# A two-block transformer forward pass on one core: the modulation vectors' operations, spread over two feed-forwards and held in VectorE's program order

## The chip, the cores and the metric

One NeuronCore of one Trainium2 chip runs the whole program. The metric is the device time of one execution in microseconds (us); the time before is the median of three runs. TensorE does the matrix products, VectorE and ScalarE the elementwise work, GpSimd a part of the elementwise work, and SyncE's queue issues the DMAs. Each engine works through its own instructions in order.

## The reference

Two transformer blocks follow each other. Block 1 (512 tokens and 16 meta tokens, width 1024) has three branches, an output projection, and a feed-forward with a squared ReLU:

```python
u = jnp.square(jax.nn.relu(rms_norm(x, norm2_w) @ w_up))     # 1024 -> 4096
return x + u @ w_down                                        # 4096 -> 1024
```

Block 2 is modulated by vectors that depend only on two inputs, `c` and `c_ctx`, not on the tokens. `m` has nine parts of 1024 values for the latent tokens, `mc` the same for 256 context tokens (of which only parts 0 to 4 are used here, since there is one layer):

```python
m  = jnp.split((jax.nn.silu(c) @ w_ada[l] + b_ada[l])[:, None, :], N_MOD, axis=-1)
mc = jnp.split(jax.nn.silu(c_ctx) @ w_ada[l] + b_ada[l], N_MOD, axis=-1)
x = _residual(x, _swiglu(_modnorm(x, g[0], m[0], m[1]), w1, w3, w2), g[1], m[2], HALF_STEP)      # first feed-forward
h_ctx = _residual(h_ctx, _swiglu(_modnorm(h_ctx, g[0], mc[0], mc[1]), w1, w3, w2), g[1], mc[2], HALF_STEP)
# then: projections with m[3], m[4]; two attentions; residual with m[5]; second feed-forward with m[6], m[7], m[8]
```

So parts 0 and 1 are wanted when block 2's first feed-forward begins, part 2 after it, and the rest later still.

## The kernel before, in words

All products are in float32 split into a high and a low part: each product is three matmuls (high by high, high by low, low by high), and every weight tile is split on the way in, the high part by ScalarE (L132), the low part by the engine that `lo_eng` names for even and odd chunks (L136; VectorE and GpSimd alternate in the stages of interest here). A weight unit is 128 output rows by 1024, in two chunks of 4 x 128 columns; three raw buffers and four split buffers are in rotation.

The class `Emitter` writes the instructions out in one order. It walks over a list of products (`_gemm`), and after each matmul it calls `tick` (L157) with an assumed time of that matmul: its columns / 2.4 + 3 ns, 216.3 ns for 512 columns. A generator that was given to `background` is advanced by one step (a slot) each time the sum of these assumed times reaches its pace; `drain` runs all that is left of it at once. After that a scheduler orders each engine's instructions anew: it may take an instruction ahead of others on its engine if its operands are there earlier in its own model, and it inserts the waits.

Block 1's feed-forward runs in four groups. In a group, eight units of `w_up` are multiplied (8 x 24 matmuls of 512 columns), each followed by `up_evac` (L1038): VectorE multiplies out of PSUM (L1045) and squares the ReLU (L1046), ScalarE writes the high part `uh`, and VectorE (odd units) or GpSimd (even units) the low part `ul` (L274). Then eight units of `w_down` are multiplied with all eight `uh`, `ul` of the group: their last of eight steps needs the output of the group's last `up_evac`. Four PSUM buffers are in rotation.

`ada_bg` (L975) computes the modulation vectors beside this feed-forward, on VectorE: 72 tiles of `w_ada` of 128 x 1024 are loaded (three buffers, SyncE's queue), and each is multiplied with silu(c) and summed along its row in one instruction (L995) that writes one column of `modc`; the first 40 tiles are also multiplied with silu(c_ctx). It has a pace of 2250 ns. At its end come the bias and the nine coefficient vectors `cf` (L1000 to L1013). Before the fourth group it is drained, and `ctx_ops` closes its pool `ad` and prepares the context tokens.

Block 2's first feed-forward (`ffn`, L1119, with tag f1) follows. It has three groups of 6, 8 and 8 hidden tiles; a tile has a unit of w1 and a unit of w3, each 24 matmuls on 258 and 24 on 512 columns, whose evacuations `e1`, `e3` end in the high part `hh` (ScalarE) and the low part `hl` (VectorE for the 512 columns, GpSimd for the 256). After a group come its products with w2, first on 256 and then on 512 columns. `f1_tail` holds the third group's products, with `update` (the residual and the next norm) beside them.

Of the kernel before, what the change touches and what calls it, by code (L numbers as in the profile page):

```python
# [6 lines left out]
F32 = mybir.dt.float32  # L7
F32R = mybir.dt.float32r
I32 = mybir.dt.int32
AF = mybir.ActivationFunctionType  # L10
ALU = mybir.AluOpType
# [3 lines left out]
D = 1024  # L15
# [243 lines left out]
def emit(tc, d, out, dbg=None, stop=None):  # L259
    nc = tc.nc  # L260
    V, A, G, T, SP = nc.vector, nc.scalar, nc.gpsimd, nc.tensor, nc.sync
    pools = Pools(tc)
    em = Emitter(tc)
# [4 lines left out]
    S = {"dram": dram}  # L268

    def act(o, i, f=AF.Copy, **kw):  # L270
        A.activation(o, i, f, **kw)

    def sub_lo(eng, lo, x, hi):
        eng.tensor_sub(lo, x, hi.bitcast(F32))  # L274
# [21 lines left out]
    def col(name, i=0, n=1):  # L296
        o = _PCOLS[name][0] + i
        return pc[:, o:o + n]
# [7 lines left out]
    def hilo(hi, lo, x, c):  # L306

        act(hi, x, scale=c)
        V.scalar_tensor_tensor(lo, x, c, hi.bitcast(F32), ALU.mult, ALU.subtract)
# [640 lines left out]
    AF0, A0C, B1X, B1C, A2X, A2C, B3, A4, B5 = range(9)  # L950

    def cf(i, k=None):
        t = S["cf"][:, i, :]
        return t if k is None else t[:, k:k + 1]

    def mod(k, s=0):
        return S["modc"][:, s, 8 * k:8 * k + 8]

    def open_f():
        for n in ("m2", "bina", "xhl"):  # L960
            pools.close(n)
        p = S["hlx"] = pools.open("hlx")
        S["XH"] = p.tile([128, KT, 514], F32R, name="XH")
        S["XL"] = p.tile([128, KT, 514], F32R, name="XL")
        S["modc"] = p.tile([128, 2, 72], F32, name="modc")
        S["cf"] = p.tile([128, 9, 8], F32, name="cf")
        S["R4"] = p.tile([128, 768], F32, name="R4")
        S["RF"] = p.tile([128, 512], F32, name="RF")
        p = S["hlc"] = pools.open("hlc")
        S["CH"] = p.tile([128, KT, 258], F32R, name="CH")  # L970
        S["CL"] = p.tile([128, KT, 258], F32R, name="CL")
        S["up"] = pools.open("up")
        S["ad"] = pools.open("ad")

    def ada_bg():  # L975

        p = S["ad"]
        sb = p.tile([128, 2, D], F32, name="sb")
        SP.dma_start(sb, d["cc"].partition_broadcast(128))
        act(sb, sb, AF.Silu)  # L980
        W, todo = [], list(range(72))

        def load():
            if todo:
                w = p.tile([128, D], F32, name="wa", tag="wa", bufs=3)
                SP.dma_start(w, d["wa"][todo.pop(0)])
                W.append(w)
        for _ in range(3):
            load()
        yield  # L990
        for j in range(72):
            w = W.pop(0)
            for s_ in ((1, 0) if j < 40 else (0,)):
                o = w if s_ == 0 else p.tile([128, D], F32, name="wx", tag="wx")
                V.tensor_tensor_reduce(o, w, sb[:, s_, :], 1.0, 0.0, ALU.mult, ALU.add,  # L995
                                       S["modc"][:, s_, j:j + 1])
                if s_ == 0:
                    load()
                yield
        V.tensor_add(S["modc"][:, 0, :], S["modc"][:, 0, :], col("bada", 0, 72))  # L1000
        V.tensor_add(S["modc"][:, 1, 0:40], S["modc"][:, 1, 0:40], col("bada", 0, 40))

        def gcol(i):
            return col("g", 8 * i, 8)
        for o, i, m_, s_ in ((AF0, 0, 1, 0), (A0C, 0, 1, 1), (A2X, 2, 4, 0), (A2C, 2, 4, 1), (A4, 4, 7, 0)):
            V.tensor_scalar_add(cf(o), mod(m_, s_), 1.0)
            V.tensor_mul(cf(o), cf(o), gcol(i))
        V.tensor_mul(cf(AF0), cf(AF0), col("final", 0, 8))
        for o, i, m_, s_, w in ((B1X, 1, 2, 0, 0.5), (B1C, 1, 2, 1, 0.5), (B3, 3, 5, 0, None), (B5, 5, 8, 0, 0.5)):
            V.tensor_mul(cf(o), mod(m_, s_), gcol(i))  # L1010
            if w is not None:
                V.tensor_scalar_mul(cf(o), cf(o), w)
        yield  # L1013

    def shift_cols(kx, kc):
        todo = [(S["XH"], S["XL"], 512 + i, mod(kx)) for i in range(2)]
        if kc is not None:
            todo += [(S["CH"], S["CL"], 0, mod(kx)), (S["CH"], S["CL"], 1, mod(kc, 1))]
        for h_, l_, o, m_ in todo:
            act(h_[:, :, o], m_)  # L1020
            sub_lo(V, l_[:, :, o], m_, h_[:, :, o])

    def ctx_ops():

        pools.close("ad")
        p = S["fp"]
        shift_cols(0, 0)
        for k in range(KT):
            c = p.tile([128, 256], F32, name="xr", tag="xr", bufs=3)
            SP.dma_start(c, d["cx"][:, k, :])  # L1030
            hilo(S["CH"][:, k, 2:258], S["CL"][:, k, 2:258], c, cf(A0C, k))
            squares(c, S["acc"][:, 0:256], k == 0, S["fpa"], G)
        tmp = S["fpa"].tile([128, 512], F32, name="sq", tag="sq", bufs=2)
        rnorm(S["R4"][:, 512:768], S["acc"][:, 0:256], D, tmp, gap=2800)
# [24 lines left out]
    def last_down(n, x):  # L1059
# [22 lines left out]
        em.after(1500, norms)  # L1082

    em.call(open_f)
    em.background(ada_bg, 2250)
    for g in range(4):
        if g == 3:
            em.drain()
# [30 lines left out]
    def ffn(tag, w1, w3, w2, mode, ntok, pool, Rk, down, head, tail):  # L1119


        st = {}
        grp = ((0, 6), (6, 8), (14, 8))

        def e1(j):
            def f(t0, n, ps, b):
                s_ = st[j, t0] = S[pool].tile([128, 512], F32, name="fs", tag="fs", bufs=3)[:, 0:n]
                V.tensor_mul(s_, ps, S[Rk][:, t0:t0 + n])  # L1128
                act(s_, s_, AF.Silu, bias=b)
            return f  # L1130

        def e3(j):
            def f(t0, n, ps, b):
                s_ = st.pop((j, t0))
                t = S[pool].tile([128, 512], F32, name="ft", tag="ft", bufs=2)
                V.tensor_mul(t[:, 0:n], ps, S[Rk][:, t0:t0 + n])  # L1136
                V.scalar_tensor_tensor(s_, t[:, 0:n], b, s_, ALU.add, ALU.mult)
                hh, hl = st["h"]
                act(hh[:, j, t0:t0 + n], s_)
                sub_lo(G if t0 else V, hl[:, j, t0:t0 + n], s_, hh[:, j, t0:t0 + n])  # L1140
            return f

        def newh():
            st["h"] = [S[pool].tile([128, KT, ntok], F32R, name="h" + e, tag="h" + e) for e in "hl"]

        for gi, (k0, nk) in enumerate(grp):
            em.call(newh)

            def pair(j, m, a=0, k0=k0):
                proj(w1[k0 + j], 128, m, e1(j), (tag, 1, a))  # L1150
                proj(w3[k0 + j], 128, m, e3(j), (tag, 3, a))

            def products(segs, gi=gi, k0=k0, nk=nk):
                for n in range(8):
                    em.gemm(w2[n][:, k0:k0 + nk, :], 128, lambda si: st["h"], segs,
                            lambda si, ps, n=n: down(gi, n, segs[si][0], segs[si][1], ps), kt=nk)

            for j in range(head(pair) if gi == 0 else 0, nk):
                pair(j, mode)
            if gi == 2:  # L1160
                tail(products)
            else:
                products([(512, 256), (0, 512)] if ntok == 768 else [(0, 512)])
# [88 lines left out]
        return 0  # L1252

    def f1_tail(products):
        products([(256, 512)])
        em.low_parts(V, V)
        em.call(lambda: shift_cols(3, 3))
        em.background(lambda: update(256, 768, S["fpa"], B1X, A2X, B1C, A2C, True), 1150)
        products([(0, 256)])
        em.drain()  # L1260

    em.call(open_f1)
    ffn("f1", d["w11"], d["w13"], d["w12"], XC, 768, "hid", "R4", f1_down, no_head, f1_tail)


# [20 lines left out]

    def open_kvp():
        pools.close("hid")
        p = S["kvp"] = pools.open("kvp")
        S["KH"] = p.tile([128, 2, 768], F32R, name="KH")  # L1290
        S["KL"] = p.tile([128, 2, 768], F32R, name="KL")
        S["Rkv"] = p.tile([128, 768], F32, name="Rkv")
        S["rkc"] = p.tile([128, 6], F32, name="rkc")
        S["akv"] = p.tile([128, 768], F32, name="akv")
        S["tmpk"] = p.tile([128, 768], F32, name="tmpk")
        S["krt"] = p.tile([32, 768], F32, name="krt")
        S["krs"] = p.tile([32, 2, 768], F32R, name="krs")
# [678 lines left out]
```

## Time and profile before

| | |
|---|---|
| median of 3 runs | 2831.26 us (2831.24 to 2832.66) |
| the profiled execution's own time | 2835.28 us |
| its span | 2833.3 us, mean granted TensorE clock 0.984 |
| TensorE matmul busy | 2736.0 us, 97% |
| TensorE weight load busy | 2405.3 us, 85% |
| VectorE busy | 1620.0 us, 57% |
| ScalarE busy | 1092.5 us, 39% |
| GpSimd busy | 849.9 us, 30% |
| DMA | 316.95 MB, mean 112 GB/s |

The busy time of TensorE is that of pipelined matmuls, so overlaps are in it. PE stands for TensorE, DVE for VectorE, ACT for ScalarE, POOL for GpSimd, SP for SyncE. A name like L995 is a line of the kernel. "<-" before an engine names what an engine's idle time ended with.

### The profile page before, as it was taken

To read this page: it belongs to the slowest core of one execution; us is meant where nothing else is said; L and a number is where in the kernel's file an instruction comes from. 1 tells how busy PE (TensorE), PEld (TensorE's weight loads), DVE (VectorE), ACT (ScalarE), POOL (GpSimd) and SP (SyncE) were. 2 spreads that over 40 slices of the span, in tenths; PEclk is the share of its full clock that TensorE was granted. 3 is DMA by queue.
4 is the path that set the end of the run, shared out by engine and by line. 5 is a ranking of instruction groups with operands and counts; after the bars stand their busy time and mean duration, and the time that the engine had idled before them with its cause. 6 is when DMAs were issued, how large, how long until landed. Compare 5 with 4: busy or idle time off the path is not lost.

```text
span 2833.3 us, 42915 instructions
## 1 busy us (share of the span) xinstructions
PE 2736.0 (97%) x16308; PEld 2405.3 (85%) x16308; DVE 1620.0 (57%) x3318; ACT 1092.5 (39%) x2201; POOL 849.9 (30%) x710
## 2 busy tenths in 40 slices
PE   9999999999999889899999999979999999899997
PEld 8889988888878667788888888868889998899897
DVE  6554422377757999555223233496576876834346
ACT  4333322445534222243222122354455665633233
POOL 0223323433324233242111112442333224323224
PEclk9999999999999999999999999989999999999998
DMA  4222222443225658332121221334643424332324
GB/s 136 73 68 91 96 97 93 129 125 102 83 93 191 205 195 295 114 108 68 53 75 60 61 66 60 93 117 156 179 102 103 133 62 162 133 97 90 93 94 127
DMA packets 115998, 316.95 MB, mean 112 GB/s; under 512 B 21680, under 2 KB 35376, under 8 KB 115536
## 3 DMA queue, kind: packets, MB, share of 16 engines
q1 hardware_dynamic: 115792, 314.21, 35.5%
q8 instruction: 129, 2.11, 0.3%
q14 instruction: 77, 0.63, 0.1%
HBM read 279.09 MB, written 13.83 MB: 103 GB/s over the span
## 4 chain that ended last, share of the span: by engine, by line
PE 80%; DVE 14%; issue 3%; ACT 2%; DMA 0%; POOL 0%; POOLq 0%; DVEq 0%; SPq 0%; ACTq 0%
PE psg L231 49%; PE pss L231 22%; DVE wlo L136 2%; DVE wa L995 2%; DVE wx L995 1%; PE pss L277 1%; PE pst L827 1%; PE pss L278 1%; PE pss L279 1%; PE pst L1731 1%; PE pst L1717 1%; PE pss L1528 1%; PE pst L824 0%; DVE ut L1045 0%; DVE mg L1224 0%
## 5 line engine op out<-in xcount | busy, mean ns | idle before, releaser
L136 POOL TENSOR_TENSOR wlo<-raw,whi 128x512 fp32r<-128x512 f32 (+1 forms) x442 | 580.1, 1313 | 1568.4 <-ACT whi L132 1527.4
L132 ACT ACTIVATE whi<-raw 128x512 fp32r<-128x512 f32 (+1 forms) x844 | 522.7, 622 | 927.8 <-PE psg L231 588.8
L136 DVE TENSOR_TENSOR wlo<-raw,whi 128x512 fp32r<-128x512 f32 (+1 forms) x402 | 314.0, 782 | 452.6 <-ACT whi L132 451.9
L231 PE MATMUL psg<-xl,whi 128*128 128x264 f32 (+2 forms) x1104 | 362.7, 329 | 0.9 <-DVE xl L403 0.9
L231 PE MATMUL psg<-xh,whi 128*128 128x264 f32 (+2 forms) x1104 | 361.4, 328 | 1.7 <-ACT whi L132 1.2
L231 PE MATMUL psg<-xh,wlo 128*128 128x264 f32 (+2 forms) x1104 | 361.7, 328 | 0.0
L231 PE MATMUL psg<-XH,whi 128*128 128x256 f32 (+3 forms) x984 | 308.2, 313 | 1.8 <-DVE ft L1136 1.0
L231 PE MATMUL psg<-XH,wlo 128*128 128x256 f32 (+3 forms) x984 | 308.2, 313 | 0.0
L231 PE MATMUL psg<-XL,whi 128*128 128x256 f32 (+3 forms) x984 | 307.8, 313 | 0.0
L231 PEld LDWEIGHTS psg<-xh,whi 128*128 128x128 f32 x1104 | 209.0, 189 | 18.8 <-ACT whi L132 1.4
L231 PEld LDWEIGHTS psg<-xl,whi 128*128 128x128 f32 x1104 | 209.1, 189 | 18.5 <-DVE xl L403 1.5
L231 PEld LDWEIGHTS psg<-xh,wlo 128*128 128x128 f32 x1104 | 209.2, 190 | 17.0 <-DVE wlo L136 0.2
L231 PE MATMUL pss<-XL,whi 128*128 128x256 f32 (+2 forms) x600 | 191.3, 320 | 6.1 <-DVE XL L1208 6.1
L231 PEld LDWEIGHTS psg<-XH,whi 128*128 128x128 f32 (+1 forms) x984 | 185.4, 188 | 11.5 <-issue 2.4
L231 PEld LDWEIGHTS psg<-XH,wlo 128*128 128x128 f32 (+1 forms) x984 | 185.8, 189 | 10.5 <-issue 0.2
L231 PEld LDWEIGHTS psg<-XL,whi 128*128 128x128 f32 (+1 forms) x984 | 185.8, 189 | 9.3
L231 PE MATMUL pss<-XH,wlo 128*128 128x256 f32 (+2 forms) x600 | 191.4, 319 | 1.2 <-DVE wlo L136 1.2
L231 PE MATMUL pss<-XH,whi 128*128 128x256 f32 (+2 forms) x600 | 190.9, 319 | 0.5 <-DVE fs L1128 0.5
L231 PEld LDWEIGHTS pss<-XL,whi 128*128 128x128 f32 x600 | 114.9, 192 | 14.3 <-DVE XL L1208 7.3
L231 PEld LDWEIGHTS pss<-XH,wlo 128*128 128x128 f32 x600 | 115.4, 192 | 10.1 <-DVE wlo L136 1.6
L231 PEld LDWEIGHTS pss<-XH,whi 128*128 128x128 f32 x600 | 114.9, 192 | 7.5 <-DVE fs L1128 0.7
L231 PE MATMUL pss<-hh,wlo 128*128 128x256 f32 (+1 forms) x296 | 101.8, 344 | 7.5 <-DVE wlo L136 7.5
(558 smaller groups left out, 6444.6 us busy)
## 6 DMA issues: line engine op xcount, KB each, us to landing
raw<-w SPq DMA_DIRECT2D x142, 512.0 KB, 3.3
raw<-wi SPq DMA_DIRECT2D x96, 512.0 KB, 3.3
wa<-wa SPq DMA_DIRECT2D x72, 512.0 KB, 4.2
raw<-wq SPq DMA_DIRECT2D x38, 512.0 KB, 3.5
raw<-wu SPq DMA_DIRECT2D x32, 512.0 KB, 4.2
raw<-wd SPq DMA_DIRECT2D x32, 512.0 KB, 4.1
raw<-wb SPq DMA_DIRECT2D x24, 512.0 KB, 3.2
raw<-wo SPq DMA_DIRECT2D x24, 512.0 KB, 4.0
```

The costliest lines, as they stand in the source:

```text
L132: s.nc.scalar.activation(h, raw, AF.Copy)
L136: eng.tensor_sub(l, raw, h.bitcast(F32))
L231: nc.tensor.matmul(out, l, r, start=(k == 0 and m == 0), stop=(k == it.kt - 1 and m == 2))
L277: T.matmul(o, wh, xh, start=first, stop=False)
L278: T.matmul(o, wh, xl, start=False, stop=False)
L279: T.matmul(o, wl, xh, start=False, stop=last)
L827: T.matmul(o, x[:, c, :], vs[:, c, :], start=False, stop=c == b and m == 1)
L995: V.tensor_tensor_reduce(o, w, sb[:, s_, :], 1.0, 0.0, ALU.mult, ALU.add, S["modc"][:, s_, j:j + 1])
L1528: T.matmul(ps[:, a:a + cw], q, k[:, c0:c0 + cw], start=m == 0, stop=m == 1)
L1717: T.transpose(ps[:, 128 * c:128 * c + 128], P_[:, 128 * (c0 + c):128 * (c0 + c) + 128], ident)
L1731: T.matmul(o[:, 0:256], v[:, c, :], x[:, c, :], start=c == 0 and m == 0, stop=c == 5 and m == 1)
```

## The change

The generator is started twice. The first time, beside block 1's feed-forward, it computes tiles 0 to 15 alone (parts 0 and 1, both inputs: 32 of the 112 operations of L995) at a pace of 8000 ns. The second time, beside block 2's first feed-forward, it computes tiles 16 to 71 (80 operations) at a pace of 4800 ns, and is drained before the products of the third group. Each call adds the bias to its own columns and makes the coefficients whose part it has. Every operation of L995 is wrapped in `keep_in_program_order`, which adds an edge without a wait behind the instruction that was written last on that engine, so that the scheduler can't issue it before that one. The loads have two buffers in place of three; the pool `ad` is opened before `up`, and stays open until `hid` is closed after block 2's first feed-forward.

```diff
+        S["ad"] = pools.open("ad")
         S["up"] = pools.open("up")
-        S["ad"] = pools.open("ad")
-
-    def ada_bg():
+
+    def ada_bg(j0, j1):
+
         p = S["ad"]
-        sb = p.tile([128, 2, D], F32, name="sb")
-        SP.dma_start(sb, d["cc"].partition_broadcast(128))
-        act(sb, sb, AF.Silu)
-        W, todo = [], list(range(72))
+        if j0 == 0:
+            S["sb"] = p.tile([128, 2, D], F32, name="sb")
+            SP.dma_start(S["sb"], d["cc"].partition_broadcast(128))
+            act(S["sb"], S["sb"], AF.Silu)
+        W, todo = [], list(range(j0, j1))
 
         def load():
             if todo:
-                w = p.tile([128, D], F32, name="wa", tag="wa", bufs=3)
+                w = p.tile([128, D], F32, name="wa", tag="wa", bufs=2)
                 SP.dma_start(w, d["wa"][todo.pop(0)])
                 W.append(w)
-        for _ in range(3):
-            load()
+        load()
+        load()
         yield
-        for j in range(72):
+        for j in range(j0, j1):
             w = W.pop(0)
             for s_ in ((1, 0) if j < 40 else (0,)):
                 o = w if s_ == 0 else p.tile([128, D], F32, name="wx", tag="wx")
-                V.tensor_tensor_reduce(o, w, sb[:, s_, :], 1.0, 0.0, ALU.mult, ALU.add,
-                                       S["modc"][:, s_, j:j + 1])
+                tc.keep_in_program_order(
+                    V.tensor_tensor_reduce(o, w, S["sb"][:, s_, :], 1.0, 0.0, ALU.mult, ALU.add,
+                                           S["modc"][:, s_, j:j + 1]))
                 if s_ == 0:
                     load()
                 yield
-        V.tensor_add(S["modc"][:, 0, :], S["modc"][:, 0, :], col("bada", 0, 72))
-        V.tensor_add(S["modc"][:, 1, 0:40], S["modc"][:, 1, 0:40], col("bada", 0, 40))
+        for s_, j2 in ((0, j1), (1, min(j1, 40))):
+            V.tensor_add(S["modc"][:, s_, j0:j2], S["modc"][:, s_, j0:j2], col("bada", j0, j2 - j0))
...
+            if j0 <= 8 * m_ < j1:
+                V.tensor_scalar_add(cf(o), mod(m_, s_), 1.0)
+                V.tensor_mul(cf(o), cf(o), gcol(i))
...
     def ctx_ops():
 
-        pools.close("ad")
         p = S["fp"]
...
-    em.background(ada_bg, 2250)
+    em.background(lambda: ada_bg(0, 16), 8000)
     for g in range(4):
         if g == 3:
             em.drain()
...
     def f1_tail(products):
+        em.drain()
         products([(256, 512)])
...
     em.call(open_f1)
+    em.background(lambda: ada_bg(16, 72), 4800)
     ffn("f1", d["w11"], d["w13"], d["w12"], XC, 768, "hid", "R4", f1_down, no_head, f1_tail)
...
     def open_kvp():
         pools.close("hid")
+        pools.close("ad")
```

## Rows read from the trace of the kernel before

**Rows 1.** The page's slices of the span: VectorE's busy tenths, TensorE's granted clock.

```profile
DVE  6554422377757999555223233496576876834346
...
PEclk9999999999999999999999999989999999999998
```

**Rows 2.** Stretches: window, length, busy PE, PEld, DVE, ACT, POOL, clock, DMA, GB/s.

```profile
884.00:1284.00 400.00, 369.50 (x1555) 294.69 (x1554) 324.96 (x470) 122.26 (x213) 147.33 (x99) 0.96 0.56 186
884.00:1143.00 259.00, 236.04 (x989) 187.48 (x987) 252.94 (x361) 68.88 (x117) 85.95 (x54) 0.95 0.69 232
1156.00:1284.00 128.00, 127.71 (x555) 103.58 (x554) 59.99 (x78) 47.03 (x79) 54.97 (x41) 1.00 0.32 101
1284.00:1790.00 506.00, 506.00 (x2858) 440.34 (x2858) 176.88 (x310) 139.69 (x242) 92.61 (x85) 1.00 0.20 63
1200.00:1240.00 40.00, 40.00 (x178) 33.08 (x177) 26.32 (x26) 13.15 (x22) 14.46 (x12) 1.00 0.31 96
```

**Rows 3.** PE's waits in 884:1284: engine, line, releaser, us, times, longest.

```profile
PE psg L231 <- ACT uh L271: 18.2, 5, 5.1
```

**Rows 4.** VectorE and PE at the first stalled turn: start us, us, instruction, idle before.

```profile
942.02 0.68 DVE L1046 SCALAR_TENSOR_TENSOR ut<-ut 128x512 f32<-128x512 f32 x1
942.63 1.21 DVE L995 CUSTOM_DVE_ANT_0 wx<-wa,sb 128x1024 f32<-128x1024 f32 x1
...
943.42 0.79 PE L231 MATMUL psg<-uh,whi 128*128 128x512 f32 x1 [4.88 <-ACT uh L271]
```

**Rows 5.** First and last matmuls of the feed-forward, by tile: ns, starts.

```profile
L231 PE MATMUL psg<-zh,whi x128: 387/389/628, 884.0 to 1227.5; 128*128 128x512 f32 x128
...
L231 PE MATMUL pss<-uh,wlo x128: 394/399/399, 952.7 to 1283.6; 128*128 128x512 f32 x128
```

**Rows 6.** The chain of waits, two undisturbed pieces: start us, us, what.

```profile
1217.42 10.88 PE psg L231 x48
...
1261.60 11.20 PE psg L231 x48
```

**Rows 7.** PE's groups of small matmuls in 884:1284: busy us, mean ns, idle.

```profile
L330 PE MATMUL pst<-ones,acc 128*128 128x1 f32 x12 | 1.6, 245 | 0.1
L349 PE MATMUL pst<-acc,ones 128*128 128x512 f32 x2 | 1.0, 592 | 0.0
L349 PE MATMUL pst<-sq,ones 128*128 128x256 f32 x2 | 0.7, 416 | 0.3 <-ACT sq L271 0.3
```

**Rows 8.** L995's operations and their loads, by tile: ns min/median/max, first and last start.

```profile
L995 DVE DVE_READ_ACCUMULATOR2_ANT modc<- x112: 74/77/85, 893.3 to 1145.5; 128x1 f32 x112
L995 DVE CUSTOM_DVE_ANT_0 wa<-wa,sb x72: 1206/1218/2319, 893.5 to 1143.3; 128x1024 f32<-128x1024 f32 x72
...
DMA to landing us min/median/max: 3.1/4.2/7.6
```

**Rows 9.** The third turn's first w_down matmul on PE.

```profile
1139.02 0.40 PE L231 MATMUL psg<-uh,whi 128*128 128x512 f32 x1
```

**Rows 10.** The fourth turn, free of L995: first w_down matmul, last ul, its reader.

```profile
1239.02 0.40 PE L231 MATMUL psg<-uh,whi 128*128 128x512 f32 x1
...
1242.30 0.69 DVE L274 TENSOR_TENSOR ul<-ut,uh 128x512 fp32r<-128x512 f32 x1 [0.70 <-ACT uh L271]
...
1244.16 0.39 PE L231 MATMUL psg<-ul,whi 128*128 128x512 f32 x1
```

**Rows 11.** Block 2's first turn: the last hl on VectorE, and its reader.

```profile
1391.42 0.69 DVE L274 TENSOR_TENSOR hl<-fs,hh 128x512 fp32r<-128x512 f32 x1 [0.70 <-ACT hh L271]
...
1394.81 0.39 PE L231 MATMUL psg<-hl,whi 128*128 128x512 f32 x1
```

**Rows 12.** VectorE's low parts by line, in 884:1284 and in 1284:1800: busy us, mean ns.

```profile
L136 DVE TENSOR_TENSOR wlo<-raw,whi 128x512 fp32r<-128x512 f32 x64 | 63.0, 985 | 27.5 <-ACT whi L132 27.5
...
L136 DVE TENSOR_TENSOR wlo<-raw,whi 128x512 fp32r<-128x512 f32 x64 | 44.3, 692 | 161.2 <-ACT whi L132 161.2
```

**Rows 13.** L995 by line in 884:1284: busy us, mean ns, idle before.

```profile
L995 DVE CUSTOM_DVE_ANT_0 wa<-wa,sb 128x1024 f32<-128x1024 f32 x72 | 104.8, 1460 | 2.6 <-DMA wa<-wa 2.0
```

More of the change, by code (lines that the diff above doesn't have):

```diff
@@ L1005, in ada_bg @@
         for o, i, m_, s_ in ((AF0, 0, 1, 0), (A0C, 0, 1, 1), (A2X, 2, 4, 0), (A2C, 2, 4, 1), (A4, 4, 7, 0)):
-            V.tensor_scalar_add(cf(o), mod(m_, s_), 1.0)
-            V.tensor_mul(cf(o), cf(o), gcol(i))
-        V.tensor_mul(cf(AF0), cf(AF0), col("final", 0, 8))
+            if j0 <= 8 * m_ < j1:
+                V.tensor_scalar_add(cf(o), mod(m_, s_), 1.0)
+                V.tensor_mul(cf(o), cf(o), gcol(i))
+                if o == AF0:
+                    V.tensor_mul(cf(o), cf(o), col("final", 0, 8))
         for o, i, m_, s_, w in ((B1X, 1, 2, 0, 0.5), (B1C, 1, 2, 1, 0.5), (B3, 3, 5, 0, None), (B5, 5, 8, 0, 0.5)):
-            V.tensor_mul(cf(o), mod(m_, s_), gcol(i))
-            if w is not None:
-                V.tensor_scalar_mul(cf(o), cf(o), w)
+            if j0 <= 8 * m_ < j1:
+                V.tensor_mul(cf(o), mod(m_, s_), gcol(i))
+                if w is not None:
+                    V.tensor_scalar_mul(cf(o), cf(o), w)
         yield
```

## The prediction

> **What bounds the kernel now.** I read the page's slices first: TensorE is the engine that is nearly always busy, so time is lost where it isn't, and VectorE is saturated in three slices around 900 to 1140 us, the one place where the granted clock of TensorE dips while another engine is full [rows 1]. Then the stretches: in block 1's feed-forward (884 to 1284 us) TensorE works 369.5 of 400 us, in block 2's first one 506 of 506. Up to 1143 us VectorE is busy 252.9 of 259 us; from 1156 us on, in the same feed-forward, 60 of 128 [rows 2]. The waits say what ends TensorE's idle time: most of it, 18.2 us in five waits, is `uh` from ScalarE [rows 3]. ScalarE isn't full, it waits for `ut`: at the first turn from w_up to w_down VectorE does the squared ReLU only at 942.02, between two operations of L995, and the matmul that needs the group's last `uh` stands 4.88 us [rows 4]. So a full VectorE delays the evacuation, and TensorE waits at the turn, where all eight outputs are needed.
>
> **What this feed-forward loses.** Its first matmul starts at 884.0, its last at 1283.6 [rows 5]; with one more spacing of 0.23 it takes 399.8 us. Undisturbed, 48 matmuls of w_up take 10.88 us and 48 of w_down 11.20 us [rows 6]. There are 32 units of 24 of each kind, 768 and 768: 16 x 10.88 = 174.1 and 16 x 11.20 = 179.2. The small matmuls between add 1.6 + 1.0 + 0.7 = 3.3 us [rows 7]. That makes 356.6 us, so 43.2 us are lost. A second way gives the same order: 400 - 369.5 = 30.5 us idle, and a mean clock of 0.96 means about 32 us at 1.2 instead of 2.4 GHz, of which the part with work in it loses half; 12.7 us are left for that, below the 16 that it could be at most [rows 2].
>
> **The change, part by part.**
>
> *80 of the 112 operations leave.* One takes 1.218 us and its accumulator read 0.077, together 1.295 [rows 8]. The 32 that stay are 41.4 us, over the first three groups, three quarters of 353.3 = 265 us: 16% of VectorE. Without L995 it is busy 47% on average (60.0 of 128), and 66% in a w_up phase (26.32 of 40) [rows 2]. That makes 82% at most, where 98% was. Below saturation TensorE waits only if an operation of L995 falls into the evacuation chain at a turn.
>
> *The order.* In the assumed time the old pace of 2250 ns would put the last reduction at the drain before group 4. VectorE began it at 1143.3 [rows 8], when TensorE was 4.3 us into the third w_down phase (from 1139.02 [rows 9]), with most of eight units, some 40 us, still to go. So the operations ran ahead of where they were written. The new edge ties each to the instruction written before it, mostly an evacuation, which waits for its product, or a low part, which waits for a split buffer. With 8000 ns the slots lie at 40 (1.5 before the first turn at 41.5), 120 and 128 (4.6 before and 3.4 behind the second at 124.6) and 208 (0.4 behind the third at 207.6, and thus behind the last `up_evac`, which is written first). None lies inside a chain.
>
> *The turn without L995* is in the trace: the fourth. Its last `ul` ends at 1242.30 + 0.69 = 1242.99, its reader starts at 1244.16, on time [rows 10]: 1.17 us to spare. One reduction inside the chain would cost 1.295 - 1.17 = 0.1 us, one at the longest seen, 2.319 + 0.077, 1.2 us [rows 8]. Three turns: 0 to 3.7 us, before a clock drop. I take 1.5 us, nearer to the lower end since no slot lies inside.
>
> *The drain before group 4.* By its assumed 249 us, 31 of 34 slots have passed; left are two reductions (2.6 us) and seven small operations, each between 0.08 (an accumulator read [rows 8]) and 0.69 us (a 512-column subtraction [rows 10]): 3.2 to 7.4 us on VectorE. Behind them wait evacuations and low parts; four PSUM buffers of 5.44 us each (24 matmuls of rows 6) are 21.8 us of cover. Cost 0.
>
> *Block 2's first feed-forward takes 80.* 80 x 1.295 = 103.6 us. 82 slots of 4800 ns are 394 of the 455 assumed us before the new drain (94 + 47 + 125.5 + 62.5 + 125.5), so it finds nothing left. In the trace that is some 427 us (455 assumed take about 493). VectorE goes from 35% (176.88 of 506 [rows 2]) to 59%; with 1.46 per reduction, the mean in the crowded stretch [rows 13], to 64%. TensorE has no idle time there to give, so nothing is gained. Its first turn has 2.70 us to spare: the last `hl` ends at 1392.11, its reader starts at 1394.81 [rows 11]; one reduction of 1.295 to 2.4 us fits in. Two turns fall into the reductions' time: 0, at most a few us if two stand in one chain.
>
> *The waits that the edge adds.* A reduction now stands in VectorE's queue until its tile has landed, and evacuations and low parts stand behind it. With two buffers a tile's load waits on SyncE's queue for the reduction two tiles earlier. Where a tile has one reduction (tiles 40 to 71) that reload has two slots, 9.6 assumed or 10.4 real us, less 1.3: 9.1 us for a landing of 4.2, 7.6 at worst, measured at 232 GB/s [rows 8, 2]. In the new place 56 tiles of 0.52 MB in 427 us add 69 GB/s to 63. Weight loads behind it on that queue are held as long as VectorE is late, some us, against four split chunks (10.9 us) of stock. Cost 0.
>
> *Fewer buffers, pool order, the split bias and coefficients*: no instruction on the path; parts 2 and up are wanted only behind the third group.
>
> **Sum.** 43.2 - 1.5 = 41.7 us. The profiled execution took 2835.28 us, so 2793.6; the median of the runs is 4.0 us lower, 2831.26 - 41.7 = 2789.6, which I forecast.
>
> **Rivals.**
>
> (a) *The turns still stall.* The edge holds an operation only behind one instruction; if that is a low part that itself went early, a reduction can slip into a chain. For it: VectorE is near full in w_up phases. Against it: at most one reduction in 8 us. Price per turn: up to 1.2 us of wait and, if the clock drops behind it, 4.2 to 5.3 us more (12.7 us, or half of 32 at most, over three turns of before); one to three turns 5.4 to 19.5 us on 2788.1: 2793 to 2808. A row that bears on it: the same low part takes 0.985 us on VectorE where L995 runs and 0.692 where it doesn't [rows 12], and L995 itself 1.46 instead of 1.218. The Trainium skill says why (SBUF — State Buffer, "Who interferes with whom"): a VectorE instruction with two SBUF inputs and a GpSimd instruction that reads SBUF shut each other out for a whole instruction. By that rule the moved reductions bring these delays to block 2's chains, 2.4 + 0.3 us against 2.70 to spare, and the sum would still be 41.7; the trace agrees in size.
>
> (b) *The change doesn't do what it says*: the reductions still bunch. At the old rate (112 in 252 us, 2.25 us each) 32 would fill 72 us and cover one of the three turns, leaving a third of the loss, 14 us; 80 would fill 180 us and cover block 2's first turn, up to 14 more: 2818.
>
> (c) *Slower than before: pinned reductions wait for their tiles.* Place: tiles 40 to 71. If a load took longer than 9.1 us from issue to landing, each pair of tiles would stretch by the excess, and TensorE with it once its stock is gone. The gain is eaten when the excess reaches 41.7 / 16 = 2.6 us per pair, a landing of 11.7; at 15 us it is 16 x 5.9 = 94 us, 2884. Against it: 7.6 is the longest landing, in a busier stretch.
>
> **How the numbers follow.** Forecast 0.78, its own range 2785 to 2796 (the turns at their best, other stages moving by 2 to 3 us, to 6 us lost); (a) 0.15; (b) 0.03; (c) 0.04. The range 2783 to 2810 takes in the forecast and (a) and leaves out (b) and (c). About 0.2%, 5.7 us, can be told from no change, so faster means below 2825.6: the forecast, (a) and nearly all of (b), 0.95; same 0.01; slower 0.04.
>
> **What would show it.** VectorE's busy share near 65% up to 1110 us, and 55 to 65% in block 2's first feed-forward; no wait of TensorE for `uh` over 1 us; granted clock 1.0 in both; w_down of group 4 ending near 1241 instead of 1284; 32 operations of L995's kind in the first, 80 in the second, evenly spaced. Wrong would be: the same stalls at the turns with fewer reductions (then another cause holds `ut`), waits of VectorE for the tiles' loads, or TensorE waits in block 2's feed-forward of the size of those that went.

## The result, and the profile after

The changed kernel takes 2798.76 us, median of 4 runs (2797.66 to 2800.65), beside 2831.96 for the kernel before: 0.9883 of it, 95% interval [0.9866, 0.9900], 33.2 us less. The forecast was 2789.6 with a range of 2783 to 2810: direction and range held, the gain is 8.5 us short of the 41.7 that were worked out.

The slices of the page, as in [rows 1]: VectorE's full stretch is gone, its work lies spread over twice the width.

```profile
DVE  6554422377755566557456563586676876834346
...
PEclk9999999999999999999999999999999999999998
```

The stretches, columns as in [rows 2]: block 1's feed-forward whole, up to the drain, around the drain and behind it, and the reductions' part of block 2's first feed-forward.

```profile
880.60:1244.90 364.30, 359.16 (x1553) 291.94 (x1552) 222.05 (x295) 123.34 (x211) 129.23 (x99) 0.99 0.39 125
```

```profile
880.60:1150.00 269.40, 269.31 (x1173) 219.18 (x1172) 168.30 (x210) 80.48 (x131) 81.30 (x63) 1.00 0.40 130
1150.00:1174.00 24.00, 18.96 (x76) 15.14 (x75) 18.48 (x46) 10.63 (x27) 9.69 (x9) 0.86 0.34 116
1174.00:1244.90 70.90, 70.90 (x308) 57.63 (x307) 35.27 (x40) 32.23 (x54) 38.24 (x27) 1.00 0.34 108
1245.00:1680.00 435.00, 435.00 (x2473) 379.19 (x2472) 257.29 (x441) 117.65 (x207) 83.76 (x71) 1.00 0.39 127
```

Up to 1150 us TensorE has no idle time, where [rows 2] had 23 us of it, and VectorE is busy 62% (168.3 of 269.4) instead of 98%. All of TensorE's idle time that is left lies in 24 us around the drain. TensorE's waits, as in [rows 3], name it; for `uh` there is none any more:

```profile
PE pst L330 <- POOL acc L921: 4.2, 1, 4.2
PE pst L349 <- DVE sq L340: 0.9, 1, 0.9
```

The operations of L995 (now L998) run from 901 to 1667 us, 32 in the first and 80 in the second feed-forward; a load lands after 5.8 us at most, where [rows 8] had 7.6.

```profile
L998 DVE CUSTOM_DVE_ANT_0 wa<-wa,sb x72: 1212/1219/2301, 909.0 to 1666.7; 128x1024 f32<-128x1024 f32 x72
L998 DVE CUSTOM_DVE_ANT_0 wx<-wa,sb x40: 1212/1219/2300, 901.6 to 1497.6; 128x1024 f32<-128x1024 f32 x40
...
DMA to landing us min/median/max: 3.1/3.4/5.8
```

The first turn, as the fourth was in [rows 10]: its first matmul starts at 926.31, the reduction at 925.97 runs 0.87 us into it, and the last `ul` ends at 930.29, 1.17 us before its reader. That is to the hundredth what the fourth turn had to spare before, and so it is at the other two turns (1.17 and 1.18 us, by the same rows).

```profile
925.97 1.21 DVE L998 CUSTOM_DVE_ANT_0 wa<-wa,sb 128x1024 f32<-128x1024 f32 x1
...
927.11 0.68 DVE L1051 TENSOR_TENSOR ut<-pss,R 128x512 f32<-128x512 f32 x1
927.82 1.08 DVE L1052 SCALAR_TENSOR_TENSOR ut<-ut 128x512 f32<-128x512 f32 x1
929.60 0.69 DVE L274 TENSOR_TENSOR ul<-ut,uh 128x512 fp32r<-128x512 f32 x1 [0.70 <-ACT uh L271]
```

```profile
931.46 0.39 PE L231 MATMUL psg<-ul,whi 128*128 128x512 f32 x1
```

```profile
927.06 1.29 POOL L136 TENSOR_TENSOR wlo<-raw,whi 128x512 fp32r<-128x512 f32 x1 [1.56 <-ACT whi L132]
```

The reduction did push the chain back: its first step, the multiply out of PSUM (L1051), starts 0.80 us after the turn's first matmul, where the other turns have 0.20. The second step, the squared ReLU (L1052), makes up for it: it takes 1.08 us here and 1.66 at the third turn, and at both it ends 0.55 to 0.56 us after the end of a low part that GpSimd began just before it. The third turn, VectorE and GpSimd:

```profile
1103.99 1.66 DVE L1052 SCALAR_TENSOR_TENSOR ut<-ut 128x512 f32<-128x512 f32 x1
```

```profile
1103.80 1.29 POOL L136 TENSOR_TENSOR wlo<-raw,whi 128x512 fp32r<-128x512 f32 x1 [1.56 <-ACT whi L132]
```

**The account between the two profiled executions**, from the first rows of a few tiles (block 1's feed-forward begins with `zh`, block 2's first one with `CH`, its products with `hh`, the latent projections with `KH`):

| piece | before, us | after, us | gain, us |
|---|---|---|---|
| up to the first `zh` | 884.0 | 880.6 | 3.4 |
| `zh` to `CH`: block 1's feed-forward | 399.8 | 364.3 | 35.5 |
| `CH` to `hh` | 105.1 | 105.0 | 0.1 |
| `hh` to `KH`: products, `update` | 557.6 | 559.4 | -1.8 |
| `KH` to the end of the span | 886.8 | 886.6 | 0.2 |

The first and the fourth line are not the change's: ahead of `zh` nothing on TensorE was moved, and the profiled execution before was 3.3 us above its own median (2835.28 against 2831.96); 557.6 and 559.4 both occur again in the experiments below, with the change in place. What is the change's is 35.5 us where 43.2 were lost; 7.7 remain, around the two waits shown above: 4.2 us for the context norm's sums and 0.9 for the spread of the same norm, with a lower clock beside them.

The first wait, in the changed kernel's chain of waits (start us, us, what), from the last reduction to the context norm's sums on TensorE:

```profile
1151.03 0.07 DVE wa L998
...
1152.95 0.10 DVE modc L1004
...
1153.79 0.90 ACT CH L271 x2
...
1156.97 3.46 DMA xr<-cx
1160.44 0.02 issue
1160.46 0.26 ACT CH L271
1160.72 2.36 DMA xr<-cx
...
1164.09 1.24 POOL acc L921
1165.33 0.04 issue
1165.38 1.01 PE pst L330 x4
```

`ctx_ops` runs behind the drain: bias, coefficient, then for eight context tiles a load (three buffers), the split with the coefficient, a square, and GpSimd's sum of the squares; four small matmuls (L330) add up what GpSimd left. They stand in TensorE's queue inside group 4's w_up, and all matmuls behind them wait. The granted clock fell with the wait: 0.86 in those 24 us, which is some 6.7 us at 1.2 instead of 2.4 GHz. Before, the context's reductions were among those that ran ahead. Two rows of the kernel before, by tile: its last `wx` operation began at 1061.7, and the context tiles were split from 1068.7 to 1155.7, 38 us before TensorE came to the sums at 1194.

```profile
L995 DVE CUSTOM_DVE_ANT_0 wx<-wa,sb x40: 1208/1215/2308, 892.2 to 1061.7; 128x1024 f32<-128x1024 f32 x40
```

```profile
L271 ACT ACTIVATE CH<-xr,cf x8: 492/494/514, 1068.7 to 1155.7; 128x256 fp32r<-128x256 f32 x8
```

### The profile page after: what moved, and what is told of

It is laid out like the page before. It is cut to its first block, busy times and chain, and to the rows that moved or that the text cites. A ratio compares the mean times of both kernels' runs of the same rounds, so it can differ in the third digit from the quotient of the medians.

```text
span 2795.9 us, 42922 instructions
## 1 busy us (share of the span) xinstructions
PE 2724.8 (97%) x16308; PEld 2401.5 (86%) x16308; DVE 1625.1 (58%) x3320; ACT 1092.8 (39%) x2201; POOL 838.7 (30%) x710
## 4 chain that ended last, share of the span: by engine, by line
PE 87%; DVE 8%; issue 2%; ACT 2%; DMA 1%; POOL 0%; POOLq 0%; SPq 0%; DVEq 0%; ACTq 0%
PE psg L231 52%; PE pss L231 26%; DVE wlo L136 1%; PE pss L277 1%; PE pst L827 1%; PE pss L278 1%; PE pss L279 1%; PE pst L1740 1%; PE pst L1726 1%; PE pss L1537 1%; PE pst L824 0%; DVE XL L1214 0%; DVE mg L1230 0%; PE pst L349 0%; ACT whi L132 0%
## 5 line engine op out<-in xcount | busy, mean ns | idle before, releaser
L136 POOL TENSOR_TENSOR wlo<-raw,whi 128x512 fp32r<-128x512 f32 (+1 forms) x442 | 566.2, 1281 | 1569.2 <-ACT whi L132 1524.0
L136 DVE TENSOR_TENSOR wlo<-raw,whi 128x512 fp32r<-128x512 f32 (+1 forms) x402 | 305.1, 759 | 432.9 <-ACT whi L132 431.8
L231 PEld LDWEIGHTS pss<-XL,whi 128*128 128x128 f32 x600 | 114.8, 192 | 14.3 <-DVE XL L1214 7.3
```

The source lines that it names most:

```text
L136: eng.tensor_sub(l, raw, h.bitcast(F32))
L231: nc.tensor.matmul(out, l, r, start=(k == 0 and m == 0), stop=(k == it.kt - 1 and m == 2))
```

## The experiments

Times are ratios to the kernel before on the same chip, with 95% intervals; "first" is the length of block 1's feed-forward, from the first `zh` to the first `CH`. The changed kernel itself was timed once more beside the last of them. The intervals of e3, e4, e5, e6 and e8 overlap the change's, so what these show is read from their traces.

| run | what | ratio | first, us |
|---|---|---|---|
| (after) | the change | 0.9883 [0.9866, 0.9900] | 364.3 |
| after_again | the same, more rounds | 0.9877 [0.9863, 0.9890] | 364.7 |
| e1 | moved, no edges | 0.9994 [0.9984, 1.0003] | 399.3 |
| e2 | edges, not moved | 0.9970 [0.9959, 0.9981] | 393.8 |
| e8 | edges on the second call only | 0.9882 [0.9865, 0.9898] | 369.3 |
| e9 | edges on the first call, and on one of the second | 0.9911 [0.9898, 0.9925] | 363.9 |
| e3 | pace 6000 | 0.9863 [0.9848, 0.9878] | 362.3 |
| e5 | six context buffers | 0.9857 [0.9842, 0.9872] | 363.1 |
| e6 | pace 2250 in block 2 | 0.9869 [0.9854, 0.9883] | 364.7 |
| e4 | late sums | 0.9855 [0.9840, 0.9869] | 361.1 |
| e7 | late sums, wide gap | 0.9840 [0.9825, 0.9854] | 356.6 |
| e10 | e7 again, more rounds | 0.9845 [0.9832, 0.9859] | 356.7 |

### The two halves of the change alone (e1, e2)

e1 takes the edges away:

```diff
-                tc.keep_in_program_order(
-                    V.tensor_tensor_reduce(o, w, S["sb"][:, s_, :], 1.0, 0.0, ALU.mult, ALU.add,
-                                           S["modc"][:, s_, j:j + 1]))
+                V.tensor_tensor_reduce(o, w, S["sb"][:, s_, :], 1.0, 0.0, ALU.mult, ALU.add,
+                                       S["modc"][:, s_, j:j + 1])
```

> The changed kernel without the order edges: 32 reductions beside block 1's feed-forward and 80 beside block 2's, at the same paces. Theory: the scheduler lets them run ahead again, so the 32 crowd into the first 70 us and VectorE is full at the first turn; TensorE loses about a third of the 43 us of before there (14 us), but the modulation is ready early and the wait for the context sums before group 4 (7.9 us with its clock drop) goes: 2798.8 + 14 - 8 = 2805 us, 2798 to 2812. Rival: the move alone is what counts and the edges do nothing for the turns: 2791 us, no wait for uh at any turn.

0.9994: no gain at all, and both expectations are wrong. The reductions' rows, by tile (columns as in [rows 8]):

```profile
L997 DVE CUSTOM_DVE_ANT_0 wa<-wa,sb x72: 1207/1224/2310, 889.4 to 1170.5; 128x1024 f32<-128x1024 f32 x72
```

All 72 tiles are done by 1172 us. The second call is written beside block 2's feed-forward, which begins at 1279, and not one of its 80 reductions ran there: their operands depend on nothing but their loads, so the scheduler took them back over a whole stage, and the kernel is that of before. e1 also has the two buffers, the other pool order and the split bias, so these bring nothing by themselves. TensorE waits 17.0 us for `uh` in six waits, against 18.2 in [rows 3].

e2 gives the kernel before the edges and nothing else, the same three lines the other way round.

> The kernel before with the order edges alone: all 112 reductions in block 1's feed-forward at 2250 ns, in program order. Theory: the load decides. In a w_up phase VectorE has 66% + 54% to do, falls some 9 us behind by each turn, and TensorE waits there as before; in w_down it catches up; the wait for the context sums comes on top: 2825 to 2842 us, no gain. Rival: the running ahead was what filled VectorE, and program order alone brings most of the gain: 2800 to 2810 us.

0.9970, 2825.61 us: 8 us faster, at the lower end of the first theory's range, though not its "no gain". VectorE has as much to do as before, in order:

```profile
881.00:1180.00 299.00, 278.73 (x1159) 221.66 (x1158) 274.54 (x381) 83.82 (x144) 101.11 (x67) 0.95 0.64 213
```

It is busy 92% of 299 us, and TensorE still waits 14.3 us for `uh`. So the move alone brings nothing, the edges alone 0.3%, both together 1.2%: the edges make the move happen, and the move makes the room.

### Which edges (e8, e9)

e8 keeps the edges of the second call alone (`if j0: tc.keep_in_program_order(ins)`).

> The changed kernel with the order edges on the second call's 80 reductions alone; the 32 beside block 1's feed-forward are free. Theory: the edges of the second call are what keeps the 80 out of block 1's feed-forward; the 32 run ahead and crowd into some 75 us, VectorE is full at the first turn alone and TensorE loses 12 to 14 us there, the wait for the context sums (7.9 us) goes because the modulation is ready early: 2803 us, 2798 to 2808. Rival: 32 reductions are too few to matter, and the edges on them only cost the late context chain: 2791 us.

As the theory said: 2801.72 us, and the free 32 fill VectorE at the first turn alone. The windows 920:960 and 960:1000 of e8:

```profile
920.00:960.00 40.00, 31.80 (x121) 23.57 (x121) 38.61 (x54) 8.85 (x16) 11.91 (x8) 0.87 0.57 187
960.00:1000.00 40.00, 40.00 (x175) 32.51 (x174) 24.62 (x43) 15.15 (x33) 15.29 (x13) 1.00 0.46 148
```

TensorE loses 369.3 - 356.6 = 12.7 us in this one turn (the last of the 32 begins at 962.46, before the second); the wait for the context sums is gone, since the modulation is there early. So the edges of the first call win 12.7 us at the turn and give back 7.7 at the sums, 5.0 us by these lengths. The ratios, 0.9882 and 0.9883, were taken on different chips with intervals of some 5 us to either side, and don't show it; e6 below, on e8's chip and with the change's first call, is 4.2 us faster than e8, of the same size, though their intervals overlap.

e9 keeps the edges of the first call and one of the second (`if j < 16 or j == 16 and s_ == 1`).

> The changed kernel with edges on the first call's 32 reductions and on the very first of the second call's 80 alone. Theory: what counts in the second call is only that it can't start before block 2's feed-forward; the edge on its first reduction holds the tile buffers and so the other 79, they crowd there as the scheduler likes, and block 2's turns absorb that: as the changed kernel, 0.986 to 0.989 of before, the first reduction of the second call behind 1240 us. Rival: the 79 free ones run ahead into block 1 or fill VectorE at a turn: 2805 to 2830 us.

The one edge does hold the 80 in block 2's feed-forward (the first begins at 1257.5), but there they crowd and fill VectorE at a turn, as the rival's second half said, and the theory's second half is wrong: 0.9911, 2806.75 us, 10 us more than with all edges on the same chip (2796.87). VectorE from 1280 to 1360, and TensorE's wait at block 2's first turn:

```profile
1280.00:1320.00 40.00, 40.00 (x232) 35.17 (x231) 39.97 (x65) 9.09 (x17) 9.10 (x7) 1.00 0.52 177
1320.00:1360.00 40.00, 33.10 (x181) 28.26 (x180) 39.68 (x69) 8.81 (x19) 10.72 (x8) 0.97 0.57 182
```

```profile
1357.82 0.58 PE L231 MATMUL psg<-hh,whi 128*128 128x256 f32 x1 [4.81 <-ACT hh L271]
```

It is the picture of block 1 before, one stage on: VectorE full, the high part late by way of ScalarE, a wait at the turn.

### How close they may stand in block 2 (e6)

```diff
-    em.background(lambda: ada_bg(16, 72), 4800)
+    em.background(lambda: ada_bg(16, 72), 2250)
```

> The changed kernel with a pace of 2250 ns in place of 4800 in block 2's first feed-forward: the 80 reductions stay in program order but crowd into the first 185 assumed us. Theory: VectorE has 35% + 54% to do there, near full, and the first turn has only 2.7 us to spare, so TensorE waits there a little, 0 to 5 us with a clock drop: 2799 to 2805 us. Rival: the distance doesn't matter in this feed-forward, its turns absorb what comes: 2797 to 2799 us, no wait of TensorE.

The rival holds: 0.9869 [0.9854, 0.9883], not slower than the change, and TensorE has no wait for `hh` or `hl`, only one of 1.0 us before a spread. VectorE is busy 160.9 of 205 us in 1245:1450, 78%. In the 30 us around the first turn it is at 84%, and well before it at 97%:

```profile
1265.00:1295.00 30.00, 30.00 (x173) 26.25 (x172) 29.25 (x49) 8.45 (x15) 8.26 (x6) 1.00 0.48 158
1330.00:1360.00 30.00, 30.00 (x168) 26.01 (x168) 25.33 (x46) 8.53 (x16) 6.50 (x6) 1.00 0.51 162
```

With the edges neither costs anything: 97% away from a turn, 84% at it. e9, without them, is at 99% at the turn and costs some 10 us. So the pace of 4800 ns isn't needed in this place, the order is; what the same load would cost in order at the turn was not run.

### The wait at the drain (e3, e5, e4, e7, e10)

e3 has a pace of 6000 ns in place of 8000 in the first call.

> The changed kernel with a pace of 6000 ns in place of 8000 in block 1's feed-forward, so that the 34 slots end at 204 assumed us instead of at the drain at 249. Theory: the chain last reductions, coefficients, context tiles, GpSimd's adds, context sums starts some 45 us earlier, TensorE's 4.2 us wait before group 4's second unit and the half clock behind it go, and the turns still don't stall: 2790 to 2793 us. Rival (the context tiles' loads with three buffers, or GpSimd's adds, are what is slow): the sums move forward with the chain and wait again: 2797 to 2800 us.

Half right: 0.9863, 2795.3 us, with no wait for the sums, but 2.9 us for `uh` at the third turn, where there was none. The last reductions and the context chain now lie there. VectorE's rows of that turn in e3:

```profile
1107.87 1.54 DVE L309 SCALAR_TENSOR_TENSOR CL<-xr,cf,CH 128x256 fp32r<-128x256 f32 x1
1109.33 1.77 DVE L136 TENSOR_TENSOR wlo<-raw,whi 128x512 fp32r<-128x512 f32 x1
1111.02 0.68 DVE L1051 TENSOR_TENSOR ut<-pss,R 128x512 f32<-128x512 f32 x1
```

The evacuation of the last product stands behind a context split and a low part that take 1.54 and 1.77 us instead of 0.48 and 0.69; GpSimd runs a `ul` from 1107.83 to 1109.13 and a low part until 1110.55. The Trainium skill's rule that a VectorE instruction with two SBUF inputs and a GpSimd instruction that reads SBUF shut each other out (SBUF — State Buffer, "Who interferes with whom") agrees with these rows. So a stall like that of rival (a) is real. What stands directly before the evacuation is the context's work; VectorE works without a break there from 1096.6 to 1112.4, and the last reduction (1102.92, 1.21 us) lies in that stretch too.

e5 gives the context tiles six buffers (`name="xr", tag="xr", bufs=6`), and with them the output projection's tiles, which share the tag and are done before this stage.

> The changed kernel with six buffers in place of three for the context tiles (xr), so that their loads land ahead of the coefficients. Theory: TensorE's wait for the context sums is the length of the whole chain after the drain, of which the two waits for tiles (0.4 and 0.9 us on ScalarE) are a small part; the scheduler also puts the sums some 16 matmuls earlier, so a wait of 3 to 6 us stays: 2797 to 2801 us. Rival: the tiles' loads are the cause, and the wait goes: 2790 to 2793 us.

Between the two: 0.9857, 2794.14 us, below the theory's range, but the wait is still there, 2.6 us, and the length of this feed-forward, 363.1 us, hardly differs. The scheduler placed the sums 16 matmuls (3.6 us) earlier, behind 42 of group 4 in place of 58, so the chain became some 3.6 + 4.2 - 2.6 = 5.2 us shorter. The loads are then well over a third of the 14.4 us from the last reduction to the sums, as the 3.46 + 2.36 us in the chain of waits above say; I had called them a small part. But a shorter chain doesn't end the wait while the sums move up with it.

e4 moves the waiter:

```diff
-        rnorm(S["R4"][:, 512:768], S["acc"][:, 0:256], D, tmp, gap=2800)
+        em.after(22000, lambda: rnorm(S["R4"][:, 512:768], S["acc"][:, 0:256], D, tmp, gap=2800))
```

> The changed kernel with the context norm's sums written 22 assumed us after the drain instead of at it, all else the same. Theory: the chain is as late as before, but TensorE meets the sums some 10 us later, when the adds are done: no wait, no clock drop, 2790 to 2793 us. Rival: the wait only moves, to the spread of the norm or to the first context evacuation of block 2: 2796 to 2800 us.

0.9855 [0.9840, 0.9869], 2792.76 us: the wait for the sums is gone, and some of the rival came true, 2.6 us for the spread that follows them (released by ScalarE's `sq`, the diagonals). e7 writes the sums 18 us after the drain and the spread 9 us after them (`em.after(18000, ...)`, `gap=9000`).

> The changed kernel with the context norm's sums written 18 assumed us after the drain and its spread 9 us after them in place of 2.8. Theory: both of TensorE's waits before it go (for the sums, and the 2.6 us for the spread that came in their place), the first feed-forward runs without a wait: 3 to 4 us under the kernel with late sums alone, 0.9845 of the kernel before, about 43 us less than it. Rival: the wait moves on to ScalarE's or VectorE's next step, and the time is that of late sums alone, 0.9855 of before.

2789.8 us, 0.9840 [0.9825, 0.9854], 44 us under the kernel before. Block 1's feed-forward in e7:

```profile
880.20:1236.80 356.60, 356.51 (x1554) 290.36 (x1553) 222.08 (x295) 122.83 (x211) 131.10 (x99) 1.00 0.40 128
```

356.6 us is the undisturbed length that the prediction summed from [rows 6, 7], to a tenth; all 43.2 us are recovered. GpSimd's last sum ends at 1164.98 there, and the sums matmul starts at 1166.52: the chain is no faster, TensorE meets it later.

The two were then run side by side in more rounds.

> The changed kernel itself, beside the one with late sums and a wide gap on the same chip: some 33 us under the kernel before, 0.988; 8 us above the other.

> The kernel with late sums and a wide gap once more, in more rounds: 0.984 to 0.9855 of before, 7 to 9 us under the changed kernel. Rival (the 8 us were the chip's spread): within 3 us of the changed kernel.

2796.87 and 2789.16 us, 7.7 us apart, the price of the wait by the first lengths (364.7 - 356.7 = 8.0). e7 is the best version found.

## Why the prediction was right or wrong

*What bounds the kernel, and the loss of 43.2 us*: right. e7 runs the stage in 356.6 us.

*The turns*: right that they would not stall, 1.5 us too dear, and lucky in one point. They have 1.17 us to spare as the fourth had, and TensorE doesn't wait there. But "none lies inside a chain" did not hold for the slot at 40: its reduction ran 0.87 us into the first turn and pushed the chain's first step back by 0.6 us. That this cost nothing is due to the GpSimd low part behind which the second step ends at every turn, which the prediction did not have. That the order was needed is shown by e8 for the first turn; by the other two its 32 reductions were done.

*Block 2's first feed-forward takes 80 at no cost*: right. No wait of TensorE from 1245 to 1752 us, VectorE at 59% (257.3 of 435), the value predicted. e6 and e9 bracket its limit at the first turn: 84% in order is free, 99% without the order is not.

*The waits that the edge adds*: right, 0.8 us of VectorE for a tile in one wait in all, no effect.

*The drain before group 4, "Cost 0"*: wrong, and the step that failed. I counted what the drain puts on VectorE (two reductions and small operations, under the cover of four PSUM buffers) and asked which evacuations stand behind them. I did not ask who waits for the vectors: `ctx_ops`, whose end is four small matmuls in TensorE's own queue, without any buffer in between. Holding the reductions back took away the context chain's head start: its splits began 125 us before the sums, now 12 us before (1153.4 and 1165.4). It cost 7.7 us; with the turns at 0 instead of 1.5 the sum is 43.2 - 7.7 = 35.5 us, as the trace has it.

*From the trace to the median*: 4.0 us between the profiled execution and the median were carried over as a constant. The medians differ by 33.2, the profiled executions by 2835.28 - 2797.99 = 37.3, since the one before had 3.4 us more ahead of this stage than the one after, at dips of the granted clock (0.98 against 1.00 in 600 to 700 us). The 2.3 us between 35.5 and 33.2 are of the size of these differences (1.8 us in `hh` to `KH`) and are not explained further.

*Rival (a)* did not occur in the change, and its reading of [rows 12] was wrong. The 0.985 us of a low part is the mean of the whole of block 1's feed-forward in the kernel before: 1.084 up to 1143 us, but still 0.843 from 1160 to 1284, where no L995 runs. In block 2's first feed-forward it stays at 0.692 after the change, with the 80 reductions beside it (53 low parts, 1245:1680), and the first turn has 2.69 us to spare, where the rival's delays would have left nothing. Only where the reductions crowd does it rise there: 0.900 in e6 (1245:1450).

*Rival (b), that the change doesn't do what it says*, got a chance of 0.03 and is what the move without edges does, in a stronger form than I had thought: not bunching in place, but running a stage ahead. *Rival (c)* didn't occur.

## What to carry to other kernels

Writing work later moves it only if something holds it there: an operation whose operands are ready early can be taken back by a scheduler that sees a free slot, so look in the trace where it really ran. When work is held back, follow its results to their last reader and not only its engine's queue; here the reader was a four-matmul sum in the bounding engine's own queue, and writing that reader later was worth as much as a fifth of the whole gain. A full engine off the critical path costs at the points where a whole group of its outputs is needed at once; measure there what is to spare (1.17 and 2.70 us here), and keep single operations in order below that.

## What the runs showed of the hardware that wasn't expected

The spare time at a turn is the same to 0.01 us in five turns of two kernels (1.17, 1.17, 1.17, 1.18, 1.17), though in one of them a reduction pushed the chain back by 0.6 us. In all five the squared ReLU ends 0.55 to 0.56 us after the end of a GpSimd low part that began before it, and takes 1.08 to 1.66 us; with GpSimd idle it takes 0.68 us in [rows 4] and 0.69 in e3 (1111.74). So it seems to be one GpSimd instruction, and not VectorE's load, that sets what is left to spare. That is read from the rows; no run moves that instruction.

In order, VectorE at 84% over the 30 us around a turn, and at 97% over 30 us away from one, held no output back from TensorE (e6).
